# Elementwise work of GpSimd done by VectorE, in a two-layer retention / DeltaNet / expert-retrieval step

## The chip, the cores and the metric

One core of a Trainium2 chip. The metric is device time of one launch in microseconds (us). Engines are written as in the profile: PE (TensorE products), PEld (its weight loads), DVE (VectorE), ACT (ScalarE), POOL (GpSimd), SP (the engine whose queue issues most transfers).

## The reference

Two token streams, a prompt of 128 tokens and a sample of 512, pass two layers of width 1024 with shared weights. A layer is a mixer (layer 0: retention and a short convolution; layer 1: gated DeltaNet and a Conformer convolution) and an expert mixer with 16384 experts:

```
def peer_ffn(h, wq, keys, u_tab, v_tab):
    q = (x @ wq).reshape(T, H_P, 2, D_KEY // 2)
    s = jnp.einsum('thpd,hpnd->thpn', q, keys)
    s1, i1 = lax.top_k(s[:, :, 0], TOPK); s2, i2 = lax.top_k(s[:, :, 1], TOPK)
    cand_i = (i1[..., :, None] * N_KEYS + i2[..., None, :])      # 128 * i1 + i2
    top_s, sel = lax.top_k(cand_s, TOPK)
    eidx = jnp.take_along_axis(cand_i, sel, axis=-1)
    gates = jax.nn.softmax(top_s)
    ...
        act = jax.nn.gelu(jnp.einsum('td,tkd->tk', xt, u_tab[et]))
        return jnp.einsum('tk,tkd->td', gt * act, v_tab[et])
```

Each token takes 8 x 16 experts; u_tab and v_tab hold 16384 rows of 1024 float32. DeltaNet needs the inverse of a triangular matrix for each chunk and head.

## The kernel before

The prompt's tile and the last of the sample's four token tiles get their experts by rows: GpSimd gathers 128 rows of u_tab, then 128 of v_tab, one 512 KB indirect transfer each, five ahead, into a pool of six row buffers (`fetch`, L1203). VectorE multiplies each u row tile by h and sums it (L1227) and adds each weighted v row tile to `gacc` (L1237). This is `peer_gather`, a generator that is advanced step by step behind other work.

The sample's other three tiles (384 tokens) go against all experts on TensorE, in 128 blocks of 128 experts ("experts of i1 = e"; a block is called an expert e below). For precision an operand is split in a high part, copied by ScalarE (L1307), and a low part, the difference (L1308); a product is then three one-pass products. There are two parts: `acts` computes gelu(U h) of a block (24 products of 384 columns, the tile A, low part `ul`) and stores it in memory; the dense stage in `peer_dense` loads it again (`w`), multiplies it by the gates (L1451), splits it (`wh`, `wl`) and the block of v_tab (`vh`, `vl`), and adds 18 products of 512 columns to `dacc`. In layer 1 62 of the 128 blocks are "fused": their activation is computed in the dense stage (`wf`).

Before the dense stage the sample's tiles pass `peer_topk` (per head: a comparison L1179, a product L1181, a sum L1182) and `gate_matrix` (per four tokens one comparison of 128x512, L1288, and three of 128x128, L1299, on VectorE; 8 products G on TensorE). `acts` and the gather of the sample's last tile run behind these, and behind the prompt's odd mixer in layer 0. The dense stage follows when all `acts` are done.

What sets the order: outside of the dense stages a scheduler orders the instructions of an engine at build time; from top-k to the end of `acts` the order of POOL alone is kept as the program writes it (`manual_schedule`, L1394), and in the dense stages that of POOL, DVE and ACT (L1424). On the chip each engine takes its instructions strictly in that order. Before the change POOL's written order holds the row transfers and the odd blocks' low parts in one sequence.

The four lines that carry the change, as they stand before:

```
self.split(hi, lo, w, (self.nc.vector, self.nc.gpsimd)[j % 2])            # L433, wq pieces
G.tensor_tensor(v4(off), v4(e1), m4(M_OFF + d * len(LEVELS) + lv), op=OP.mult)   # L935
self.split(uh, ul, ur, self.nc.gpsimd if e % 2 else self.nc.vector)       # L1317
self.split(vh, vl, vr, G if e % 2 else V)                                 # L1450
```

Of the kernel before, what the change touches and what calls it, by code (L numbers as in the profile page):

```python
# [17 lines left out]
P = 128  # L18
# [66 lines left out]
class Kern:  # L85
# [35 lines left out]
    @contextmanager  # L121
    def using(self, **kw):
        """these attributes for a while"""
        old = {k: getattr(self, k) for k in kw}
        self.__dict__.update(kw)
        yield
        self.__dict__.update(old)

    def laned(self, gen, **kw):
        """a generator that runs with these attributes"""  # L130
        while True:
            with self.using(**kw):
                r = next(gen, self)
                kw = {k: getattr(self, k) for k in kw}
            if r is self:
                return
            yield
# [4 lines left out]
    def all_banks(self):  # L142
        """the banks of the lane that is through, too"""
# [15 lines left out]
    def mm(self, out, lhsT, rhs, start, stop):  # L159
        """a float32 product; background work goes in between at its rate"""  # L160
# [3 lines left out]
    def tick(self, us):  # L164
        """background work for a time that the foreground takes"""
# [18 lines left out]
    def phase(self, side="left", **n):  # L184
        """scratch memory of one phase; the next phase's takes its place"""
# [13 lines left out]
    def a2(self, st, name):  # L199
        """one value per channel and token of the stream, channels on partitions"""  # L200
# [28 lines left out]
    # ---------------------------------------------------------------- helpers  # L229
    def rsqrt(self, src, scale, n, name, post=1.0):  # L230
        """post * (src * scale + EPS) ** -0.5 on a [128, n] tile, by a Newton step."""
# [12 lines left out]
    def log1p_exp_neg(self, x, n, name):  # L244
        """log(1 + exp(-|x|)) on a [128, n] tile."""
# [20 lines left out]
    def bcast_cols(self, cols, name, out=None, bank=None):  # L266
        """[128, 8] per-channel columns -> [128, 1024], the same row on each partition."""
# [11 lines left out]
    # ---------------------------------------------------------------- constants  # L279
# [47 lines left out]
    # ---------------------------------------------------------------- modulation  # L327
# [6 lines left out]
    def modulation(self, l, part):  # L334
        """Columns of sh1, sc1 (part 0), ga1 (1), sh2, sc2 (2), ga2 (3), a step for 128 of them"""
# [30 lines left out]
    def load_c_rows(self, mw):  # L366
        """2 silu(c) of both streams, the same row on each partition"""
# [10 lines left out]
    # ---------------------------------------------------------------- norm, modulate, transpose  # L378
    def normed(self, st):
        """1 / rms of the rows of the token tiles, a column each"""  # L380
# [12 lines left out]
    def h_transposed(self, st, mod, alloc, rows=None):  # L393
        """modulated rmsnorm of x as 8 tiles [128 channels, T]"""
# [27 lines left out]
    def proj_t(self, st, hT, w):  # L422
        """[128 columns of w, T] in PSUM from a piece [128, 8 x 128]"""
# [6 lines left out]
    def split_piece(self, w, j):  # L430
        """a piece's two parts"""
        hi, lo = (self.ph[t][0].tile([P, D], F32R, tag=t, name=self.nm(t)) for t in ("wh", "wl"))
        self.split(hi, lo, w, (self.nc.vector, self.nc.gpsimd)[j % 2])  # L433
        return hi, lo

    def proj_split(self, h, w):
        """proj_t with both operands split"""
# [6 lines left out]
    def proj_n(self, st, hT, ws, it):  # L444
        """[128 tokens, 512] in PSUM from four pieces [128, 2 x 512]"""
# [7 lines left out]
    def out_proj(self, st, yT, w_out, ga, cs=range(KC), its=None):  # L453
        """x += ga * (y @ w_out); a step for the first half of the chunks cs"""
# [23 lines left out]
    def taps(self, out, src, w, T, order):  # L478
        """out += w[:, j] * src shifted by j - len(w) // 2, tokens outside of the stream being 0"""
# [14 lines left out]
    # ---------------------------------------------------------------- even mixer  # L494
    def even_setup(self, ctx):
# [21 lines left out]
        # decay of the prompt's keys towards the final states, per token and (dir, head)  # L517
# [8 lines left out]
    def decay(self, st, h):  # L526
        """both directions' decay of head h between tokens, by their distance"""
# [124 lines left out]
    def even_states(self, st, kT, v):  # L652
        """final states of the prompt, both directions"""
# [18 lines left out]
    # ---------------------------------------------------------------- odd mixer  # L672
# [13 lines left out]
    def odd_mixer(self, st, ph=None):  # L686
        nc, A = self.nc, self.A
        V, S, PE, G = nc.vector, nc.scalar, nc.tensor, nc.gpsimd
# [5 lines left out]
        if big:  # L694
            # x waits in memory for the end of the mixer; k and v take its place
# [4 lines left out]
        # conformer branch: its gated projection and, behind the rest, its convolution  # L700
# [19 lines left out]
        # gates  # L720
# [16 lines left out]
        # q, k, v: short convolution and silu (twice the value) with channels on partitions, then  # L737
        # per token tile: normalised q, k, v with tokens on partitions, q and k transposed too
# [81 lines left out]
    def conformer_products(self, ys, hc, T):  # L820
        """the same on the tensor engine, a diagonal matrix for each tap"""
# [50 lines left out]
    def gdn(self, st, kn, vn, qT, kT, gg, beta, zg, of, conf, out):  # L872
        nc = self.nc
        V, S, G = nc.vector, nc.scalar, nc.gpsimd
# [12 lines left out]
        def pre(d, it, res):  # L887
            """what the scan needs of a chunk: u, w^T, decayed q^T and k, the masked attention"""
# [29 lines left out]
            G.tensor_tensor(v4(x), v4(x), m4(M_INCL + d), op=OP.mult)  # L918
            yield
            # A and the attention  # L920
# [10 lines left out]
            # (I + A)^-1 by doubling of its diagonal blocks: X holds it, Y its transpose  # L931
            Y, X = self.vt("Y"), self.vt("Xi")
            for lv, bsz in enumerate(LEVELS):
                off = self.vt("off")
                G.tensor_tensor(v4(off), v4(e1), m4(M_OFF + d * len(LEVELS) + lv), op=OP.mult)  # L935
# [113 lines left out]
    def gdn_out(self, of, zg, its):  # L1049
        """o -> its norm, gate and transpose, in place: [128 channels of a head, (head, token)]"""  # L1050
# [21 lines left out]
    # ---------------------------------------------------------------- PEER  # L1072
    def peer_prep(self, st, l):
# [4 lines left out]
        if st.s:  # L1078
# [3 lines left out]
            for c in range(KC):  # L1082
                self.split(full[0][c], full[1][c], hT[c], (self.nc.vector, self.nc.gpsimd)[c % 2])
# [4 lines left out]
        for jg in range(4):  # L1088
# [3 lines left out]
            for j in range(4 * jg, 4 * jg + 4):  # L1092
                w = self.piece(A["wq"][l, j])
                b = self.proj_split(full, self.split_piece(w, j)) if st.s else self.proj_t(st, hT, w)
# [638 lines left out]
```

## Time and profile before

| what | us |
|---|---|
| median of 3 timed runs | 4401.43 (4391.63 to 4402.98) |
| span of the profiled execution, the only time recorded of it | 4406.5 |
| PE busy / DVE busy / POOL busy / ACT busy in it | 3868.7 / 3677.7 / 2411.8 / 1498.3 |

The times are device times of whole launches; the profile is one further execution, whose span reads 0.1% above the median. "Busy" is time in which an engine had an instruction running. An instruction's span in a timeline can overlap that of the next on its engine by some 0.1 us; where instructions follow one another without idle time, the distance of two starts is what one costs.

### The profile page before, as it was taken

The numbers are of one execution on the slowest core, as the hardware profiler recorded it, in microseconds if no ns is written. First come the engines' busy times: TensorE is split into PE (matmuls) and PEld (weight loads), VectorE is DVE, ScalarE is ACT, GpSimd is POOL, SyncE is SP. The second block draws the span as 40 slices with busy tenths as digits, with TensorE's granted clock in tenths as the row PEclk, the third lists the DMA queues.
The fourth block names the chain that finished last, engine by engine and source line by source line (L and its number), as shares of the span: only waits on it lengthen the run. The fifth ranks groups of instructions, "written<-read, shape, count | busy, mean of one in ns | idle before, by whom it ended". The sixth has DMA issues, their size and how long they took to land.

```text
span 4406.5 us, 56677 instructions
## 1 busy us (share of the span) xinstructions
PE 3868.7 (88%) x19422; PEld 3206.9 (73%) x19422; DVE 3677.7 (83%) x6843; ACT 1498.3 (34%) x2828; POOL 2411.8 (55%) x1520
## 2 busy tenths in 40 slices
PE   6797858899999998899998987887589989999997
PEld 4453547899998987677775456756579978888886
DVE  6568889998998656988887997659989978888888
ACT  2110131122774442233332253532224743333333
POOL 0126673686143754766655777425265247776664
PEclk9998878789999999999999989899899999999999
DMA  7548886886688788899987967237256699989994
GB/s 284 172 157 328 288 305 232 310 316 228 237 301 304 246 284 307 269 320 319 320 304 278 339 225 236 65 120 253 72 202 224 256 321 327 326 311 319 322 318 171
DMA packets 437040, 1158.45 MB, mean 263 GB/s; under 512 B 39440, under 2 KB 188048, under 8 KB 430352
## 3 DMA queue, kind: packets, MB, share of 16 engines
q1 hardware_dynamic: 282064, 591.69, 38.5%
q0 software_dynamic: 154688, 563.15, 36.3%
q8 instruction: 152, 2.49, 0.2%
q14 instruction: 136, 1.11, 0.1%
HBM read 1060.71 MB, written 93.98 MB: 262 GB/s over the span
## 4 chain that ended last, share of the span: by engine, by line
PE 31%; DVE 16%; issue 10%; POOL 3%; ACT 2%; DMA 2%; SPq 0%; DVEq 0%; POOLq 0%; ACTq 0%
PE dacc L161 14%; PE A L161 10%; DVE row L1227 3%; DVE gacc L1237 3%; POOL row L1203 2%; PE po L161 2%; PE G L161 1%; DVE wl L1308 1%; ACT wh L1307 1%; DMA row<-v,eid 1%; DMA row<-u,eid 1%; PE pt L161 1%; DVE ul L1308 1%; DVE eq L1179 1%; DVE o L1299 1%
## 5 line engine op out<-in xcount | busy, mean ns | idle before, releaser
L161 PE MATMUL A<-hHL,uh 128*128 128x384 f32 x4096 | 1110.4, 351 | 25.9 <-ACT uh L1307 25.7
L1203 POOL DMA_INDIRECT row<-v,eid x512 | 672.9, 1314 | 491.3 <-DVE gacc L1237 195.7
L1227 DVE SCALAR_TENSOR_TENSOR row<-row,hn 128x1024 f32<-128x1024 f32 x512 | 701.3, 1385 | 153.5 <-DMA row<-u,eid 151.8
L1203 POOL DMA_INDIRECT row<-u,eid x512 | 688.0, 1344 | 249.9 <-DVE row L1227 110.3
L161 PEld LDWEIGHTS A<-hHL,uh 128*128 128x128 f32 x4096 | 767.9, 196 | 40.0 <-ACT uh L1307 28.4
L1237 DVE SCALAR_TENSOR_TENSOR gacc<-row,gel,gacc 128x1024 f32<-128x1024 f32 x508 | 744.6, 1466 | 55.3 <-DMA row<-v,eid 50.6
L161 PE MATMUL A<-hHL,ul 128*128 128x384 f32 x2048 | 721.0, 353 | 65.4 <-DVE ul L1308 59.8
L1308 POOL TENSOR_TENSOR ul<-ur,uh 128x1024 fp32r<-128x1024 f32 x128 | 334.1, 2610 | 504.0 <-ACT uh L1307 456.0
L161 PE MATMUL dacc<-vh,wh 128*128 128x512 f32 x1536 | 458.7, 397 | 77.2 <-ACT wh L1307 77.1
L1308 POOL TENSOR_TENSOR vl<-vr,vh 128x1024 fp32r<-128x1024 f32 x128 | 355.3, 2776 | 267.9 <-ACT vh L1307 146.3
L161 PE MATMUL dacc<-vl,wh 128*128 128x512 f32 x1536 | 474.9, 392 | 1.3 <-POOL vl L1308 1.3
L161 PE MATMUL dacc<-vh,wl 128*128 128x512 f32 x1536 | 457.9, 390 | 7.9 <-DVE wl L1308 7.9
L1307 ACT CAST wh<-w 128x384 fp32r<-128x384 f32 (+1 forms) x226 | 133.0, 589 | 963.6 <-DVE w L1451 422.0
L161 PEld LDWEIGHTS A<-hHL,ul 128*128 128x128 f32 x2048 | 400.8, 196 | 79.1 <-DVE ul L1308 67.2
L161 PE MATMUL pt<-hT,w 128*128 128x128 f32 (+1 forms) x1664 | 395.6, 395 | 22.9 <-DMA w<-wq 11.6
L1307 ACT CAST uh<-ur 128x1024 fp32r<-128x1024 f32 x256 | 267.7, 1046 | 422.5 <-PE A L161 288.6
L161 PEld LDWEIGHTS dacc<-vh,wh 128*128 128x128 f32 x1536 | 282.1, 189 | 161.2 <-ACT wh L1307 110.6
L161 PEld LDWEIGHTS pt<-hT,w 128*128 128x128 f32 x1664 | 246.4, 199 | 164.6 <-issue 143.8
L161 PEld LDWEIGHTS dacc<-vh,wl 128*128 128x128 f32 x1536 | 287.7, 188 | 73.3 <-DVE wl L1308 11.4
L161 PEld LDWEIGHTS dacc<-vl,wh 128*128 128x128 f32 x1536 | 288.4, 188 | 60.4 <-POOL vl L1308 2.6
L1307 ACT CAST vh<-vr 128x1024 fp32r<-128x1024 f32 x256 | 267.2, 1044 | 4.5 <-DMA vr<-v 4.4
L1451 DVE TENSOR_TENSOR w<-w,gt 128x384 f32<-128x384 f32 x194 | 243.8, 1257 | 3.7 <-DMA w<-wd 3.7
(373 smaller groups left out, 6160.3 us busy)
## 6 DMA issues: line engine op xcount, KB each, us to landing
ur<-ut SPq DMA_DIRECT2D x256, 512.0 KB, 4.6
vr<-v SPq DMA_DIRECT2D x256, 512.0 KB, 6.7
gd<-gst SPq DMA_DIRECT2D x48, 1024.0 KB, 5.7
gt<-gd SPq DMA_DIRECT2D x96, 512.0 KB, 7.8
wd<-w SPq DMA_DIRECT2D x194, 192.0 KB, 3.8
w<-wd SPq DMA_DIRECT2D x194, 192.0 KB, 6.4
w<-ada_k SPq DMA_DIRECT2D x56, 512.0 KB, 6.4
w<-wq SPq DMA_DIRECT2D x48, 512.0 KB, 5.3
```

Source lines behind the costliest of these rows:

```text
L161: self.nc.tensor.matmul(out, lhsT, rhs, start=start, stop=stop)
L1179: V.tensor_tensor(eq, sf[:, h, :].unsqueeze(2).to_broadcast([P, TOPK, NSLOT]), self.iota50.unsqueeze(1).to_broadcast([P, TOPK, NSLOT]), op ...
L1203: self.nc.gpsimd.indirect_dma_start(out=t, out_offset=None, in_=table, in_offset=bass.IndirectOffsetOnAxis(ap=idx, axis=0))
L1227: V.scalar_tensor_tensor(u, u, 1.0, hn, op0=OP.mult, op1=OP.mult, accum_out=act[:, k:k + 1])
L1237: V.scalar_tensor_tensor(gacc, v, t[:, k:k + 1], gacc, op0=OP.mult, op1=OP.add)
L1299: V.tensor_scalar(o1, self.iota128, cols[:, 0, t:t + 1], cols[:, 2, t:t + 1], op0=OP.is_equal, op1=OP.mult)
L1307: self.nc.scalar.copy(hi, src)
L1308: (eng or self.nc.vector).tensor_tensor(lo, src, hi.bitcast(F32), op=OP.subtract)
L1451: V.tensor_tensor(w.rearrange("p (b t) -> p b t", t=TB), w.rearrange("p (b t) -> p b t", t=TB), g[:, :, e % GQ, :], op=OP.mult)
```

## The change

Every elementwise instruction of GpSimd is issued on VectorE, with the same operands and shapes. GpSimd keeps the row transfers and the plain transfers of the prompt's weights. `split` loses its engine argument. (The diff also empties docstrings and comments, which changes no instruction.)

```
-    def split(self, hi, lo, src, eng=None):
+    def split(self, hi, lo, src):
         self.nc.scalar.copy(hi, src)
-        (eng or self.nc.vector).tensor_tensor(lo, src, hi.bitcast(F32), op=OP.subtract)
+        self.nc.vector.tensor_tensor(lo, src, hi.bitcast(F32), op=OP.subtract)
...
-        self.split(hi, lo, w, (self.nc.vector, self.nc.gpsimd)[j % 2])
+        self.split(hi, lo, w)
...
-                self.split(full[0][c], full[1][c], hT[c], (self.nc.vector, self.nc.gpsimd)[c % 2])
+                self.split(full[0][c], full[1][c], hT[c])
...
-        self.split(uh, ul, ur, self.nc.gpsimd if e % 2 else self.nc.vector)
+        self.split(uh, ul, ur)
...
-                self.split(vh, vl, vr, G if e % 2 else V)
+                self.split(vh, vl, vr)
...
-            nc.gpsimd.tensor_tensor(eq, eq, ci[:, h, :].unsqueeze(1).to_broadcast([P, TOPK, NSLOT]), op=OP.mult)
+            V.tensor_tensor(eq, eq, ci[:, h, :].unsqueeze(1).to_broadcast([P, TOPK, NSLOT]), op=OP.mult)
...
-            G.tensor_tensor(v4(x), v4(x), m4(M_INCL + d), op=OP.mult)
+            V.tensor_tensor(v4(x), v4(x), m4(M_INCL + d), op=OP.mult)
...
-                G.tensor_tensor(v4(off), v4(e1), m4(M_OFF + d * len(LEVELS) + lv), op=OP.mult)
+                V.tensor_tensor(v4(off), v4(e1), m4(M_OFF + d * len(LEVELS) + lv), op=OP.mult)
```

Three places show what this does to the orders. In the dense stage of layer 0, DVE, an even and an odd block (`vl` the low part of the v block, `gacc` the gather's sum, `w` the gates' product). Before:

```order
L1308 TENSOR_TENSOR vl_15011<-vr_14865,vh_15010 128x1024
L1451 TENSOR_TENSOR w_14867<-w_14867,gt_14727 128x384
L1308 TENSOR_TENSOR wl_15016<-w_14867,wh_15015 128x384
L1237 SCALAR_TENSOR_TENSOR gacc_13277<-row_14869,gel_13274,gacc_13277 128x1024
L1451 TENSOR_TENSOR w_14901<-w_14901,gt_14727 128x384
L1308 TENSOR_TENSOR wl_15051<-w_14901,wh_15050 128x384
```

And of the change:

```order
L1308 TENSOR_TENSOR vl_15011<-vr_14865,vh_15010 128x1024
L1451 TENSOR_TENSOR w_14867<-w_14867,gt_14727 128x384
L1308 TENSOR_TENSOR wl_15016<-w_14867,wh_15015 128x384
L1237 SCALAR_TENSOR_TENSOR gacc_13277<-row_14869,gel_13274,gacc_13277 128x1024
L1308 TENSOR_TENSOR vl_15046<-vr_14899,vh_15045 128x1024
L1451 TENSOR_TENSOR w_14901<-w_14901,gt_14727 128x384
L1308 TENSOR_TENSOR wl_15051<-w_14901,wh_15050 128x384
```

The odd block's `vl` now stands on DVE ahead of its `w`; nothing else moved there.

POOL behind the prompt's odd mixer of layer 0, rows of u_tab (`u,eid`) for the sample's last tile. Before:

```order
L1203 DMA row_12738<-u,eid_4955 128x1024
L1203 DMA row_12787<-u,eid_4955 128x1024
L1203 DMA row_12790<-u,eid_4955 128x1024
L1308 TENSOR_TENSOR ul_12805<-ur_12753,uh_12804 128x1024
L1203 DMA row_12836<-u,eid_4955 128x1024
L1203 DMA row_12908<-u,eid_4955 128x1024
L1203 DMA row_12911<-u,eid_4955 128x1024
L1308 TENSOR_TENSOR ul_12929<-ur_12874,uh_12928 128x1024
```

And of the change:

```order
L1203 DMA row_12738<-u,eid_4955 128x1024
L1203 DMA row_12787<-u,eid_4955 128x1024
L1203 DMA row_12790<-u,eid_4955 128x1024
L1203 DMA row_12836<-u,eid_4955 128x1024
L1203 DMA row_12908<-u,eid_4955 128x1024
L1203 DMA row_12911<-u,eid_4955 128x1024
```

Before, every third row transfer stood behind a low part, which needs its block's `uh` from ScalarE; now the row transfers stand behind one another alone.

DVE in the gate matrix of layer 0 (`o` the comparisons of L1288 and L1299, `row,act` a gathered u row tile's product). Before:

```order
L1299 TENSOR_SCALAR o_1470_7087<-iota_98,gcols_6887 128x128
L1299 TENSOR_SCALAR o_1471_7090<-iota_98,gcols_6887 128x128
L1299 TENSOR_SCALAR o_1472_7093<-iota_98,gcols_6887 128x128
L1288 TENSOR_TENSOR o_1468_7084<-iota_98,gcols_6887 128x512
L1308 TENSOR_TENSOR ul_7461<-ur_7253,uh_7460 128x1024
L1299 TENSOR_SCALAR o_1476_7104<-iota_98,gcols_6887 128x128
L1299 TENSOR_SCALAR o_1477_7107<-iota_98,gcols_6887 128x128
L1299 TENSOR_SCALAR o_1478_7110<-iota_98,gcols_6887 128x128
L1288 TENSOR_TENSOR o_1474_7101<-iota_98,gcols_6887 128x512
```

And of the change, the same tokens:

```order
L1299 TENSOR_SCALAR o_1470_7087<-iota_98,gcols_6887 128x128
L1299 TENSOR_SCALAR o_1471_7090<-iota_98,gcols_6887 128x128
L1299 TENSOR_SCALAR o_1472_7093<-iota_98,gcols_6887 128x128
L1227 SCALAR_TENSOR_TENSOR row_10019,act_5108<-row_10019,hn_2873 128x1024
L1227 SCALAR_TENSOR_TENSOR row_10074,act_5108<-row_10074,hn_2873 128x1024
L1227 SCALAR_TENSOR_TENSOR row_10077,act_5108<-row_10077,hn_2873 128x1024
L1299 TENSOR_SCALAR o_1476_7104<-iota_98,gcols_6887 128x128
L1299 TENSOR_SCALAR o_1477_7107<-iota_98,gcols_6887 128x128
L1288 TENSOR_TENSOR o_1474_7101<-iota_98,gcols_6887 128x512
L1299 TENSOR_SCALAR o_1478_7110<-iota_98,gcols_6887 128x128
```

The scheduler has placed gathered row products among the comparisons that stood behind the gate matrix before. Counted in the whole order of layer 0, between the first and the last comparison of the gate matrix DVE has 21 row products and 12 `ul` before, and 95 and 34 of the change; between the first L1179 and the gate matrix 20 row products and 50 `gacc` before, 33 and 43 of the change; behind the gate matrix, up to the dense stage, 87 row products before and none of the change. On PE, 66.7 blocks of `acts` stand ahead of the gate matrix's last product before and 72.5 of the change, 44.9 and 41.1 ahead of its first.

## Rows read from the trace of the kernel before

**Rows 1.** The page, part 1: busy us of each engine, share of the span.
```profile
PE 3868.7 (88%) x19422; PEld 3206.9 (73%) x19422; DVE 3677.7 (83%) x6843; ACT 1498.3 (34%) x2828; POOL 2411.8 (55%) x1520
```

**Rows 2.** Stages: length; busy us, (instructions); granted clock, DMA share, GB/s.
```profile
811.00:1110.00 299.00, 280.59 (x1602) 278.37 (x1602) 267.62 (x448) 71.38 (x102) 216.51 (x119) 0.86 0.78 277
1110.00:1315.00 205.00, 193.21 (x1361) 187.90 (x1359) 199.20 (x458) 149.90 (x338) 63.11 (x36) 1.00 0.75 271
1315.00:1749.00 434.00, 405.62 (x2559) 386.83 (x2559) 294.66 (x736) 170.34 (x315) 213.95 (x140) 0.97 0.81 286
1749.00:2346.00 597.00, 538.19 (x2277) 421.41 (x2276) 524.94 (x477) 188.54 (x266) 378.47 (x191) 1.00 0.86 294
2605.00:2870.00 265.00, 210.03 (x1431) 180.71 (x1429) 195.66 (x245) 124.39 (x288) 164.59 (x123) 0.88 0.42 139
2960.00:3590.00 630.00, 510.84 (x2927) 474.72 (x2926) 577.49 (x1538) 270.92 (x525) 291.16 (x167) 0.92 0.61 212
3590.00:4395.00 805.00, 783.26 (x3773) 684.53 (x3771) 704.38 (x681) 275.91 (x399) 547.30 (x306) 1.00 0.87 303
```

**Rows 3.** Groups of POOL: busy us, mean ns | idle before, releaser.
```profile
L1308 POOL TENSOR_TENSOR vl<-vr,vh 128x1024 fp32r<-128x1024 f32 x128 | 355.3, 2776 | 267.9 <-ACT vh L1307 146.3 <-issue 116.3 <-DVE wl L1308 4.8
L1308 POOL TENSOR_TENSOR ul<-ur,uh 128x1024 fp32r<-128x1024 f32 x128 | 334.1, 2610 | 504.0 <-ACT uh L1307 456.0 <-PE G L161 27.9 <-PE A L161 20.1
L1181 POOL TENSOR_TENSOR eq<-eq,ci 128x800 f32<-128x800 f32 x80 | 166.3, 2081 | 119.4 <-DVE eq L1179 103.0 <-DVE eid L1187 11.8 <-DVE ci L1164 3.5
L935 POOL TENSOR_TENSOR off<-e,msk 128x512 f32<-128x512 f32 x70 | 102.7, 1484 | 34.3 <-PE bY L161 12.3 <-DVE hc L869 10.5 <-DVE e L928 6.3
```

**Rows 4.** Timeline, DVE, two blocks of layer 0: start us, us.
```profile
2000.57 0.56 DVE L1308 TENSOR_TENSOR wl<-w,wh 128x384 fp32r<-128x384 f32 x1 [0.62 <-ACT wh L1307]
...
2003.38 0.55 DVE L1451 TENSOR_TENSOR w<-w,gt 128x384 f32<-128x384 f32 x1
2004.55 0.56 DVE L1308 TENSOR_TENSOR wl<-w,wh 128x384 fp32r<-128x384 f32 x1 [0.62 <-ACT wh L1307]
2005.03 1.28 DVE L1237 SCALAR_TENSOR_TENSOR gacc<-row,gel,gacc 128x1024 f32<-128x1024 f32 x1
2006.22 2.80 DVE L1451 TENSOR_TENSOR w<-w,gt 128x384 f32<-128x384 f32 x1
2009.64 0.56 DVE L1308 TENSOR_TENSOR wl<-w,wh 128x384 fp32r<-128x384 f32 x1 [0.62 <-ACT wh L1307]
```

**Rows 5.** Timeline, POOL, the same stretch.
```profile
2005.60 3.00 POOL L1308 TENSOR_TENSOR vl<-vr,vh 128x1024 fp32r<-128x1024 f32 x1 [1.33 <-issue]
```

**Rows 6.** Timeline, PE, the same stretch.
```profile
2005.26 0.62 PE L161 MATMUL dacc<-vl,wh 128*128 128x512 f32 x2
...
2008.43 0.61 PE L161 MATMUL dacc<-vh,wl 128*128 128x512 f32 x2
```

**Rows 7.** Groups of DVE over the span.
```profile
L1227 DVE SCALAR_TENSOR_TENSOR row<-row,hn 128x1024 f32<-128x1024 f32 x512 | 701.3, 1385 | 153.5 <-DMA row<-u,eid 151.8 <-DVE row L1227 0.4
L1451 DVE TENSOR_TENSOR w<-w,gt 128x384 f32<-128x384 f32 x194 | 243.8, 1257 | 3.7 <-DMA w<-wd 3.7
...
L1308 DVE TENSOR_TENSOR wl<-wf,wh 128x384 fp32r<-128x384 f32 x62 | 166.8, 2690 | 41.5 <-ACT wh L1307 41.5
```

**Rows 8.** Timeline, DVE, gate matrix of layer 0.
```profile
1191.99 0.85 DVE L1299 TENSOR_SCALAR o<-iota,gcols 128x128 f32<-128x128 f32 x3
...
1193.36 1.22 DVE L1308 TENSOR_TENSOR ul<-ur,uh 128x1024 fp32r<-128x1024 f32 x1
...
1197.24 2.89 DVE L1299 TENSOR_SCALAR o<-iota,gcols 128x128 f32<-128x128 f32 x3
```

**Rows 9.** Timeline, POOL, the same stretch.
```profile
1196.60 2.95 POOL L1308 TENSOR_TENSOR ul<-ur,uh 128x1024 fp32r<-128x1024 f32 x1 [17.92 <-ACT uh L1307]
```

**Rows 10.** Waits of DVE, 1315 to 1749 us: total us, times, longest.
```profile
DVE row L1227 <- DMA row<-u,eid: 71.7, 42, 10.0
```

**Rows 11.** Waits, scan of layer 1 (2605 to 2870 us).
```profile
PE bY L492 <- DVE Xi L937: 26.0, 8, 6.9
```

More of the change, by code (lines that the diff above doesn't have):

```diff
@@ L428, in proj_t, with split_piece @@
         return b
-    def split_piece(self, w, j):
+    def split_piece(self, w):
         hi, lo = (self.ph[t][0].tile([P, D], F32R, tag=t, name=self.nm(t)) for t in ("wh", "wl"))
-        self.split(hi, lo, w, (self.nc.vector, self.nc.gpsimd)[j % 2])
+        self.split(hi, lo, w)
         return hi, lo
@@ L687, in odd_mixer @@
         nc, A = self.nc, self.A
-        V, S, PE, G = nc.vector, nc.scalar, nc.tensor, nc.gpsimd
+        V, S, PE = nc.vector, nc.scalar, nc.tensor
         T, nt = st.T, st.nt
@@ L873, in gdn @@
         nc = self.nc
-        V, S, G = nc.vector, nc.scalar, nc.gpsimd
+        V, S = nc.vector, nc.scalar
         nt = st.nt
@@ L1093, in peer_prep @@
                 w = self.piece(A["wq"][l, j])
-                b = self.proj_split(full, self.split_piece(w, j)) if st.s else self.proj_t(st, hT, w)
+                b = self.proj_split(full, self.split_piece(w)) if st.s else self.proj_t(st, hT, w)
                 q = self.a2(st, "q")
@@ L1358, in peer_dense @@
         nc, A = self.nc, self.A
-        V, S, PE, G = nc.vector, nc.scalar, nc.tensor, nc.gpsimd
+        V, S, PE = nc.vector, nc.scalar, nc.tensor
         tiles, gt = list(range(st.nt - 1)), st.nt - 1
```

## Prediction

> **What bounds the kernel now.** I read the busy times first: PE 88%, DVE 83%, POOL 55% [rows 1]. These are means over stages with different limits, so I cut the span into stages [rows 2] and asked in each which engine is full. Layer 0: in the top-k stage (811 to 1110 us) PE has 281 of 299 us and DVE 268; in the gate matrix (1110 to 1315) 193 and 199 of 205; in the prompt's odd mixer (1315 to 1749) PE has 406 of 434 and DVE only 295; in the dense stage (1749 to 2346) PE 538 and DVE 525 of 597. Layer 1: the scan (2605 to 2870) fills neither; split, top-k and gate matrix (2960 to 3590) fill DVE (577 of 630); the dense stage (3590 to 4395) fills PE (783 of 805).
>
> Then I looked at what a POOL instruction does to DVE. In the dense stage of layer 0 the gates' product `w` of an even block takes 0.55 us; that of the odd block starts at 2006.22, while POOL works on `vl` (2005.60 to 2008.60), and takes 2.80, to 2009.02 [rows 4, 5]. 2008.60 plus 0.55 is 2009.15, within 0.13: the short instruction runs when POOL's is over. In the gate matrix three comparisons take 0.85 us, and 2.89 when POOL's `ul` runs from 1196.60 to 1199.55 [rows 8, 9]. So DVE and POOL's elementwise work take turns, and much of DVE's busy time is waiting inside instructions: `w` over the span has a mean of 1257 ns against 550, `wl` of fused blocks 2690 against 560, the row product 1385 against about 1200 [rows 4, 7]. That is 194 x 0.71 = 137, 62 x 2.13 = 132 and 512 x 0.19 = 95 us, 364 together, without the groups not shown.
>
> **What the change moves.** POOL loses 128 `vl`, 128 `ul`, 80 `eq` products and 70 `off` masks [rows 3], and 34 smaller ones. On DVE a difference of 128x1024 takes 1.22 us [rows 8]; by width I take 0.96 for 800 columns and 0.65 for 512 (estimates, not above 1.22 nor below 0.55, the 384 columns of `w`). 256 x 1.22 + 80 x 0.96 + 70 x 0.65 + 34 x about 0.9 = 465 us are added, at least 364 given back: DVE's total hardly moves, so where the work comes to stand decides. Each wait is now for a smaller reason, but the order also changes: row transfers no longer stand behind POOL's `ul`, which waited for `uh` (504 us idle ahead of `ul` [rows 3]), and the scheduler has moved 74 more row products into the gate matrix of layer 0. By stage:
>
> Dense, layer 0. An even block's round on DVE is 3.98 us (`wl` at 2000.57 to `wl` at 2004.55), an odd one's 5.09 (to 2009.64) [rows 4]; the mean is 4.53. With its own `vl` the odd round becomes an even one, 3.98. PE needs 18 products at (2008.43 - 2005.26) / 14 = 0.226 us [rows 6], 4.08. PE then sets the pace. Transfers take 0.86 of the DMA engines now [rows 2], and would take 0.94 at the new pace; I take 4.12. The first 24 blocks stand beside the prompt's top-k: (597 - 104 x 4.53) / 24 = 5.2 us each, with eight more `eq` products and 12 more `vl` on DVE against what they blocked; I take no change. 104 x 0.41 = **-43**. Ends: -21, if transfers hold it at 4.33, and -55, if the first blocks gain too.
>
> Gate matrix, layer 0. One group of four tokens costs DVE 1.37 us (1191.99 to 1193.36) [rows 8], 96 groups 132. Before: 21 row products x 1.2 (the distance 2005.03 to 2006.22 of its sister `gacc` [rows 4]) = 25, 12 `ul` = 14, 12 stalls of 2.0 = 24, sum 195 of 205, rest 10. Now: 132 + 95 x 1.2 + 34 x 1.2 + 10 = 297, and I add 3 for late rows: 300, **+95**. The 74 transfers that come with them (POOL has nothing else to do there) bring 38 MB; with 55 MB now and 8 more blocks' loads that is about 99 MB in 300 us, 330 GB/s, above every stage of rows 2. Ends: +80 and +130.
>
> Top-k, layer 0. Added to DVE: 32 x 0.96 + 22 x 1.22 + 13 row products x 1.2 - 7 `gacc` x 1.2 = 65. Given back: 54 stalls, between 0.85 us (the 364 over 426 instructions) and 2.0 each; with DVE 90% busy most POOL instructions hit one, and I take 1.4, 75. The sum's hand-over from POOL is gone too: **-18** (ends -43, +20; PE has 3.8 blocks less here).
>
> Odd mixer, layer 0. PE is full, and has 61.3 - 55.5 = 5.8 blocks less to do, because they ran beside the long gate matrix: 5.8 x 24 products x 0.17 (0.226 by width) = 24 us. DVE loses 87 row products and their 71.7 us of waiting [rows 10], which PE's work covered: little comes of it. **-27** (ends -45, -15).
>
> Scan, layer 1. 56 masks and 8 others move to DVE, 64 x 0.65 = 42 us, against 64 stalls of some 0.65. On the chain a mask of 1.48 us [rows 3] becomes 0.65 once in each of seven levels, in two waves of chunks: 7 x 2 x 0.83 = 12; PE's 26 us behind `Xi` [rows 11] may shrink too. What is queued behind a mask on DVE is the next `gacc`, 1.28. **-12** (ends -25, +10).
>
> Split, top-k, gate matrix, layer 1. 32 x 0.96 + 33 x 1.22 + 12 x 1.1 = 84 added, 77 stalls x 1.2 = 92 back: **-8** (ends -45, +20). Here only a dozen row products change places.
>
> Dense, layer 1. PE has 22 us of idle time, no more can come: **-10** (ends -18, 0). DVE gets 95 x 1.2 = 114 and gets back the 132 of `wl` alone.
>
> What lies ahead of 811 us and between 2346 and 2605 moves next to nothing: **0**. Sum: -43 + 95 - 18 - 27 - 12 - 8 - 10 = -23. The profile's span is 4406.5, 5 us above the median of the runs; the difference is taken to the median: 4401 - 23 = **4378**.
>
> One rule speaks against the change. The Trainium skill, "Perfetto Trace Analysis", Optimizing Scalar/DVE Operations, says that offloading from a saturated DVE, even to GPSIMD, may make sense, and adds that the two share an SBUF read port, so that it might not help. By its first half the 465 us would simply lengthen the stages in which DVE is full; rows 4 and 5, where 3.00 us of POOL cost DVE 2.25, bear out the second half.
>
> **The rivals.**
> (A) Slower: the row products in the gate matrix wait for their rows. In the odd mixer 87 of them waited 71.7 us, 0.82 each [rows 10], beside idle time; in the gate matrix such a wait holds every comparison behind it. 95 x 0.82 = 78: the sum becomes +55, 4456. It decides from 0.38 us a row on (36 us). For it: 330 GB/s. Against it: rows now leave POOL at once, five ahead, one per 3 us.
> The Trainium skill, "SBUF — State Buffer", SBUF: two separate sides, has a rule that would feed this: a DVE instruction in a two-port mode keeps GPSIMD from writing the descriptors of its transfers. No row here shows such a stall.
> (B) The dense stages are held by transfers: 4.33 a block in layer 0 (-21 in place of -43) and nothing in layer 1: -23 + 22 + 10 = +9, 4410.
> (C) The gate matrix gives more back: ends of three terms, +80, -43, -45: -23 - 15 - 25 - 18 = -81, 4320. For it: PE's idle 28 us in the odd mixer.
> (D) DVE's long instructions are its own, and nothing is given back: +65, +119, +77 (64 x 1.2 in the dense stage), +42 and +84 by stage, less 27: +360, 4761. Rows 4, 5, 8 and 9 are against it.
>
> **How the numbers follow.** My forecast 0.50, A 0.18, B 0.13, C 0.17, D 0.02. The forecast's own range is 4348 to 4408. The range for 8 in 10 reaches from C's time into A's, 4318 to 4440. A measurement tells about 0.3%, 13 us. Faster: 0.38 of the forecast, C, 0.01 of B: 0.56. Same: 0.09 and 0.10 of B: 0.19. Slower: 0.03, A, 0.02 of B, D: 0.25.
>
> **What the profile after would show.** Right: `w` at 0.55 and `wl` at 0.56 in all blocks; 4.1 us a block in layer 0's dense stage with PE without gaps; a gate matrix of some 300 us in layer 0, full on DVE, with PE idle in it; DVE's total below 3700. Wrong: long instructions on DVE with no POOL work beside them; waits for `row<-u` in the gate matrix above 36 us; a gate matrix under 270 us; DMA share at its limit in the dense stages.

## The result, and the profile after

The changed kernel takes 4282.4 us (median of 4 runs, 4273.4 to 4289.4) against 4397.1 (4 runs): ratio 0.973, 95% interval 0.970 to 0.976. The medians are 115 us apart; the profiled execution has a span of 4287.3 us, 119.2 below that of before, and since stages can be read from profiles alone, I go by these 119 us. I had forecast 4378, with a range from 4318 up: the sign was right, the size far too small.

The page, part 1, of the changed kernel (busy us, share of the span):

```profile
PE 3831.8 (89%) x19422; PEld 3202.6 (75%) x19422; DVE 3467.9 (81%) x7283; ACT 1506.8 (35%) x2825; POOL 1475.3 (34%) x1080
```

DVE has 440 more instructions and 210 us less busy time than in [rows 1]. The stages, cut at the same events as in [rows 2]:

```profile
820.00:1092.00 272.00, 257.51 (x1536) 255.24 (x1537) 258.41 (x533) 67.48 (x96) 126.54 (x83) 0.89 0.92 331
1092.00:1372.00 280.00, 244.34 (x1543) 234.28 (x1542) 271.11 (x602) 161.88 (x352) 130.14 (x91) 0.95 0.93 341
1372.00:1763.00 391.00, 377.07 (x2456) 361.28 (x2455) 192.66 (x611) 161.45 (x305) 1.64 (x2) 0.99 0.58 189
1763.00:2295.00 532.00, 519.34 (x2274) 425.55 (x2272) 452.49 (x543) 192.97 (x256) 220.29 (x120) 1.00 0.94 329
2552.00:2787.00 235.00, 204.22 (x1451) 177.08 (x1450) 194.31 (x312) 126.41 (x293) 78.60 (x59) 0.92 0.48 158
2877.00:3485.00 608.00, 505.42 (x2923) 475.24 (x2922) 549.63 (x1617) 266.81 (x524) 118.22 (x90) 0.91 0.62 220
3485.00:4275.00 790.00, 779.71 (x3779) 682.16 (x3777) 623.48 (x769) 279.09 (x397) 306.39 (x212) 1.00 0.89 309
```

Only the second, the gate matrix of layer 0, became longer (205 to 280): DVE is full (271 of 280) and PE idle for 36 us. The stage behind it gives back 43. Groups of DVE over the span:

```profile
L1237 DVE SCALAR_TENSOR_TENSOR gacc<-row,gel,gacc 128x1024 f32<-128x1024 f32 x508 | 650.9, 1281 | 31.3 <-DMA row<-v,eid 27.6
L1227 DVE SCALAR_TENSOR_TENSOR row<-row,hn 128x1024 f32<-128x1024 f32 x512 | 612.9, 1222 | 62.2 <-DMA row<-u,eid 60.3
L1451 DVE TENSOR_TENSOR w<-w,gt 128x384 f32<-128x384 f32 x194 | 107.4, 554 | 3.7 <-DMA w<-wd 3.7
...
L1181 DVE TENSOR_TENSOR eq<-eq,ci 128x800 f32<-128x800 f32 x80 | 78.1, 990 | 0.0
...
L935 DVE TENSOR_TENSOR off<-e,msk 128x512 f32<-128x512 f32 x70 | 45.2, 688 | 0.0
...
L1308 DVE TENSOR_TENSOR wl<-wf,wh 128x384 fp32r<-128x384 f32 x62 | 34.6, 559 | 39.4 <-ACT wh L1307 39.4
```

Against [rows 7] `w` fell from 1257 to 554 ns and `wl` of fused blocks from 2690 to 559. `gacc` fell from 1466 to 1281, 94 us over its 508, a group I had left out of the sum. Two blocks of the dense stage of layer 0, the timeline of DVE (start us, us), beside [rows 4]:

```profile
2000.93 0.56 DVE L1308 TENSOR_TENSOR wl<-w,wh 128x384 fp32r<-128x384 f32 x1 [0.62 <-ACT wh L1307]
2001.40 1.28 DVE L1237 SCALAR_TENSOR_TENSOR gacc<-row,gel,gacc 128x1024 f32<-128x1024 f32 x1
2002.62 1.23 DVE L1308 TENSOR_TENSOR vl<-vr,vh 128x1024 fp32r<-128x1024 f32 x1
2003.76 0.55 DVE L1451 TENSOR_TENSOR w<-w,gt 128x384 f32<-128x384 f32 x1
2004.94 0.56 DVE L1308 TENSOR_TENSOR wl<-w,wh 128x384 fp32r<-128x384 f32 x1 [0.62 <-ACT wh L1307]
...
2009.02 0.56 DVE L1308 TENSOR_TENSOR wl<-w,wh 128x384 fp32r<-128x384 f32 x1 [0.62 <-ACT wh L1307]
```

The odd block now takes an even block's time: 4.01 and 4.08 us from one `wl` to the next, where they were 3.98 and 5.09. Waits of DVE in the gate matrix (1092 to 1372 us): total, times, longest.

```profile
DVE row L1227 <- DMA row<-u,eid: 3.0, 3, 1.9
```

95 waits of 0.82 us were rival A's price; DVE waited 3.0 us in all. The rows came in time.

### The profile page after: what moved, and what is told of

It is laid out like the page before. It is cut to its first block, busy times and chain, and to the rows that moved or that the text cites. A ratio compares the mean times of both kernels' runs of the same rounds, so it can differ in the third digit from the quotient of the medians.

```text
span 4287.3 us, 56379 instructions
## 1 busy us (share of the span) xinstructions
PE 3831.8 (89%) x19422; PEld 3202.6 (75%) x19422; DVE 3467.9 (81%) x7283; ACT 1506.8 (35%) x2825; POOL 1475.3 (34%) x1080
## 4 chain that ended last, share of the span: by engine, by line
PE 63%; DVE 16%; issue 7%; DMA 4%; POOL 3%; ACT 1%; SPq 0%; DVEq 0%; POOLq 0%; ACTq 0%
PE dacc L161 23%; PE A L161 20%; PE pt L161 7%; DVE row L1227 3%; POOL row L1203 3%; PE G L161 2%; PE mod L347 2%; PE po L161 2%; PE cy L161 1%; DVE o L1299 1%; DMA row<-u,eid 1%; DMA row<-v,eid 1%; DVE gacc L1237 1%; DVE ul L1308 1%; DVE o L1288 1%
## 5 line engine op out<-in xcount | busy, mean ns | idle before, releaser
L1203 POOL DMA_INDIRECT row<-v,eid x512 | 745.5, 1456 | 1460.6 <-DVE gacc L1237 713.2
L1203 POOL DMA_INDIRECT row<-u,eid x512 | 700.3, 1368 | 1048.6 <-DVE row L1227 641.3
L1237 DVE SCALAR_TENSOR_TENSOR gacc<-row,gel,gacc 128x1024 f32<-128x1024 f32 x508 | 650.9, 1281 | 31.3 <-DMA row<-v,eid 27.6
L1227 DVE SCALAR_TENSOR_TENSOR row<-row,hn 128x1024 f32<-128x1024 f32 x512 | 612.9, 1222 | 62.2 <-DMA row<-u,eid 60.3
L161 PE MATMUL dacc<-vh,wh 128*128 128x512 f32 x1536 | 480.4, 394 | 31.4 <-ACT wh L1307 31.3
L1308 DVE TENSOR_TENSOR ul<-ur,uh 128x1024 fp32r<-128x1024 f32 x256 | 312.7, 1223 | 166.6 <-ACT uh L1307 166.4
L161 PE MATMUL dacc<-vh,wl 128*128 128x512 f32 x1536 | 391.2, 390 | 0.0
L1308 DVE TENSOR_TENSOR vl<-vr,vh 128x1024 fp32r<-128x1024 f32 x256 | 313.2, 1224 | 72.2 <-ACT vh L1307 69.8
L1308 DVE TENSOR_TENSOR wl<-w,wh 128x384 fp32r<-128x384 f32 (+1 forms) x226 | 147.0, 652 | 110.8 <-ACT wh L1307 110.6
```

The source lines that it names most:

```text
L161: self.nc.tensor.matmul(out, lhsT, rhs, start=start, stop=stop)
L1203: self.nc.gpsimd.indirect_dma_start(out=t, out_offset=None, in_=table, in_offset=bass.IndirectOffsetOnAxis(ap=idx, axis=0))
L1227: V.scalar_tensor_tensor(u, u, 1.0, hn, op0=OP.mult, op1=OP.mult, accum_out=act[:, k:k + 1])
L1237: V.scalar_tensor_tensor(gacc, v, t[:, k:k + 1], gacc, op0=OP.mult, op1=OP.add)
L1308: self.nc.vector.tensor_tensor(lo, src, hi.bitcast(F32), op=OP.subtract)
```

## The experiments

My theory (theory 1 in the expectations): DVE and GpSimd take turns at elementwise work, so what GpSimd does costs DVE about as much as doing it itself would, or more; the 119 us are these stalls less the added work, and beside that the change moved the row products to a worse place. Rivals: GpSimd's results only came late to those who wait for them (hand-over); or the order of the instructions made the gain.

The table has the lengths of stages in us, from each profiled execution, between the starts of the same instructions: first `eq` of layer 0's sample, first and last one-hot comparison (L1299), first and last `w` of the dense stage; last row product to last `cy` of layer 1's mixer; layer 1's first `wl` to its first dense `w`. So some differ by up to 23 us from the windows above. The first mixers, up to the split of layer 0, vary from 584 to 604 us among these executions, which is why I compare stages. Of the totals I compare ratios to before, with their 95% intervals.

| run | top-k 0 | gate 0 | odd mixer 0 | sum of three | dense 0 | scan 1 | split to gate 1 | ratio |
|---|---|---|---|---|---|---|---|---|
| before | 304 | 200 | 435 | 940 | 594 | 243 | 628 | 1 |
| changed | 276 | 276 | 391 | 943 | 528 | 212 | 606 | 0.973 (0.970-0.976) |
| e1 pace | 243 | 240 | 464 | 946 | 516 | 211 | 613 | 0.976 (0.973-0.979) |
| e2 idle subtraction | 274 | 275 | 391 | 941 | 619 | 211 | 608 | 0.994 (0.991-0.996) |
| e3 `vl` back | 272 | 275 | 391 | 938 | 586 | 210 | 607 | 0.985 (0.982-0.989) |
| e4 `ul` back | 264 | 214 | 449 | 928 | 528 | 208 | 612 | 0.973 (0.970-0.976) |
| e5 masks back | 274 | 202 | 434 | 911 | 528 | 238 | 608 | 0.973 (0.970-0.976) |
| e6 `eq` back | 276 | 277 | 407 | 959 | 538 | 209 | 627 | 0.986 (0.983-0.988) |
| e7 idle copy | 273 | 275 | 391 | 939 | 565 | 209 | 608 | 0.978 (0.975-0.981) |
| e8 `ul` of layer 0 back | 260 | 212 | 449 | 921 | 528 | 211 | 608 | 0.969 (0.966-0.972) |
| e9 pace, 72 blocks | 251 | 237 | 435 | 923 | 528 | 209 | 607 | 0.966 (0.963-0.969) |
| e10 prompt's masks back | 274 | 207 | 433 | 915 | 528 | 206 | 604 | 0.963 (0.961-0.966) |
| e11 before, `vl` moved | 301 | 200 | 429 | 930 | 538 | 244 | 629 | 0.985 (0.982-0.989) |
| e12 idle in the scan | 271 | 274 | 391 | 937 | 528 | 235 | 606 | 0.977 (0.974-0.980) |

### Idle work on GpSimd: e2, e7, e12

The edits are shown against the changed kernel, cut to the lines that matter; what stands behind `#` is mine.

```diff
                 self.split(vh, vl, vr)
+                if l == 0 and e & 1:
+                    nc.gpsimd.tensor_tensor(st.hn, st.hn, st.hn, op=OP.subtract)   # e2
+                    nc.gpsimd.tensor_copy(st.hn, st.hn)                            # e7, in its place
```

e2. 

> All of the change stays; in the dense stage of layer 0, each odd block gets one GpSimd subtraction of 128x1024 on a tile that is no longer read (`hn`, from itself), so no instruction waits for it. The order on DVE is that of the changed kernel. Theory 1 (turn-taking): each of the 64 costs DVE up to 2.25 us in the instruction that meets it; DVE has 458 of 531 us there, so up to 64 x 2.25 = 144 are added, and the stage goes to 458 + 144 = 602 at most, 570 to 602: 4282 + 40 to 70 = 4320 to 4350, with `w` or `vl` of about 3 us in odd blocks. Rival (hand-over: what cost time was that `vl` and `ul` of GpSimd came 1.5 us later than DVE's; a product that nobody waits for costs nothing): 4282, within 5, and no long instruction on DVE.

e7. 

> As the run e2, but each of the 64 idle pieces of GpSimd work is a copy of 128x1024 with one operand (`hn` onto itself) in place of a subtraction with two. If all elementwise work of GpSimd takes turns with DVE: the dense stage of layer 0 goes from 528 towards 619 us as in e2, and `wl` of odd blocks takes 2 us: 4282 + 97 = 4379, less in the ratio of the two durations. Rival (only two-operand work of GpSimd takes turns with DVE's): 4282, within 6, `wl` at 0.56.

e2 took the dense stage from 528 to 619 us and the kernel to 4379.1. DVE's timeline and then GpSimd's in e2, one odd block, and the group of `wl` in that stage (a mean of 1242 ns, where it was 559):

```profile
2007.19 2.08 DVE L1308 TENSOR_TENSOR wl<-w,wh 128x384 fp32r<-128x384 f32 x1 [0.62 <-ACT wh L1307]
```

```profile
2006.94 1.90 POOL L1452 TENSOR_TENSOR hn<-hn 128x1024 f32<-128x1024 f32 x1
```

```profile
L1308 DVE TENSOR_TENSOR wl<-w,wh 128x384 fp32r<-128x384 f32 x126 | 156.5, 1242 | 70.6 <-ACT wh L1307 70.6
```

GpSimd's instruction ends at 2008.84, `wl` at 2009.27, 0.43 later: it ran when the other was through. 56 of the 64 odd blocks read like this one; the instruction that was met is `wl`, not the `w` or `vl` of my expectation. Nobody waits for `hn`, so hand-over cannot be the cause here; 64 x (2.08 - 0.56) = 97 is near the 91 that the stage lost. The stage went past my upper bound of 602, which let the stalls fill DVE's idle time; that idle time (72 us in the changed kernel, 70 in e2) is the 0.62 that DVE waits for `wh` in every block, and it stays. In e7 (4312.9 us) the same block reads, DVE and then GpSimd:

```profile
2007.03 1.20 DVE L1308 TENSOR_TENSOR wl<-w,wh 128x384 fp32r<-128x384 f32 x1 [0.63 <-ACT wh L1307]
```

```profile
2006.76 1.05 POOL L1452 COPY hn<-hn 128x1024 f32<-128x1024 f32 x1
```

A copy takes turns too: it ends at 2007.81, and `wl` 0.42 later, as in e2. Its price is 64 x 0.64 = 41 (measured 36), less than in the ratio of the two durations, because both pieces start some 0.26 us ahead of `wl` and only what is left of them counts. The rival, that only two-operand work of GpSimd counts, falls. The Trainium skill, "SBUF — State Buffer", Who interferes with whom, says that a DVE instruction with two SBUF inputs contends with a GpSimd instruction that reads SBUF. `wl` has two inputs, and both idle pieces read: the rows of e2 and e7 agree.

```diff
                 V.tensor_tensor(v4(off), v4(e1), m4(M_OFF + d * len(LEVELS) + lv), op=OP.mult)
+                if st.s:
+                    nc.gpsimd.tensor_tensor(st.hn[:, :512], off, off, op=OP.subtract)
```

e12. 

> All of the change stays; in layer 1's mixer, behind each of the 56 masked products `off` on DVE, GpSimd makes one idle subtraction of 128x512 of `off` from itself, onto a tile that is no longer read, and nothing waits for it but the buffer of `off`. The masks' own length on the chain of the inversion stays 0.69 us. If the scan gained because GpSimd's masks held DVE (and their queue the row transfers), most of the 31 us comes back: scan 211 to 230 or more, 4282 + 20 = 4302. Rival (the gain was the mask's shorter length and hand-over on the chain, 1.48 against 0.69 us and no semaphore between two engines): scan 211 to 215, 4282 to 4286.

The scan went to 235, the kernel to 4309.2. Two groups of DVE in e12's scan, in the changed kernel 1283 and 689 ns:

```profile
L1239 DVE SCALAR_TENSOR_TENSOR gacc<-row,gel,gacc 128x1024 f32<-128x1024 f32 x65 | 97.9, 1507 | 11.3 <-DMA row<-v,eid 10.7 <-DVE off L935 0.2
L935 DVE TENSOR_TENSOR off<-e,msk 128x512 f32<-128x512 f32 x56 | 49.0, 917 | 0.0
```

Work off the chain takes away 23 of the 31 us that the scan had gained. The masks' own length and hand-over, on which my forecast had rested, are left with about 8, if the idle pieces cost DVE what the masks did; PE's waits for a mask, 12.3 us before and 3.8 after, say the same.

### One part undone, or done alone: e3, e4, e5, e6, e11

`split` gets its engine argument again in e3 and e4.

```diff
-                self.split(vh, vl, vr)
+                self.split(vh, vl, vr, nc.gpsimd if e % 2 else V)        # e3
...
-        self.split(uh, ul, ur)
+        self.split(uh, ul, ur, self.nc.gpsimd if e % 2 else self.nc.vector)   # e4
...
-            V.tensor_tensor(v4(x), v4(x), m4(M_INCL + d), op=OP.mult)
+            nc.gpsimd.tensor_tensor(v4(x), v4(x), m4(M_INCL + d), op=OP.mult)   # e5, and L935 alike
...
-            V.tensor_tensor(eq, eq, ci[:, h, :].unsqueeze(1).to_broadcast([P, TOPK, NSLOT]), op=OP.mult)
+            nc.gpsimd.tensor_tensor(eq, eq, ci[:, h, :].unsqueeze(1).to_broadcast([P, TOPK, NSLOT]), op=OP.mult)   # e6
```

e3. 

> From the changed kernel, the `vl` subtractions of odd blocks go back to GpSimd (128), all else stays. Theory 1: the dense stage of layer 0 goes back from 531 to about 590 us (4.54 a block), that of layer 1 gains at most 5 (PE 788 of 793, DVE 626 - 78 + 60 of stalls): 4282 + 60 = 4342, ratio to before 0.986. Rival (the dense stage gained from the row transfers or from the start that the other moves gave it): under 4310.

It took 4337.0: `vl` alone is worth 1.2% (54 us), all of it in layer 0's dense stage (528 to 586).

e11, the same part alone, on the kernel before:

```diff
-                self.split(vh, vl, vr, G if e % 2 else V)
+                self.split(vh, vl, vr, V)
```

> From the kernel before, `vl` of the odd blocks alone (128) goes to DVE, all else stays on GpSimd. By the dense stage of layer 0 (594 to about 535: 3.98 to 4.08 us a block in the steady part) and nothing in layer 1 (there `ul` still takes turns, and PE has 12 us of idle time): 4401 - 58 = 4343, ratio 0.987. Rival (the parts of the change need each other: the `ul`, `eq` and masks that stay take the gain): above 4370.

It took 4340.5 against 4407.9. This part does not need the others; I had missed 11 us in layer 1's dense stage (790 to 780 between first and last `w`).

e4. 

> From the changed kernel, the `ul` subtractions of odd blocks go back to GpSimd (128), and with them the order of the rows before the change (17 + 20 row products up to the end of the gate matrix). Theory 1: it costs 128 stalls of 1 to 2 us less 128 x 1.22 of DVE work; in layer 0 the better order gives back what the stalls take: top-k, gate matrix and odd mixer 943 to 930, layer 1's top-k + 15, dense + 5: 4282 + 5, from 4270 to 4300. Against e1, which has the same order without stalls, + 30 (15 to 45). Rival (order alone): as e1 within 6 us. Rival (the gain came from `ul`, which left GpSimd's queue and no longer held the rows): above 4320.

It took 4284.4, as the changed kernel: a loss and a gain that cancel. But e4 was no slower than e1, which has the same row order and no stalls of `ul`; that part of the expectation (+30) failed, and e1 and e9 below show why.

e5. 

> From the changed kernel, the 70 products with a mask of the inversion's levels (`off`) and the 10 of `X` go back to GpSimd, all else stays. Theory 1, with GpSimd's queue in it (a mask stands behind a row transfer that waits for DVE's sum `gacc`, and DVE is held by the masks in turn): the scan of layer 1 goes back from 211 to 243 us, the rest stays: 4282 + 31 = 4313, from 4304 to 4322. Rival (the masks cost only their own length on the chain, 7 levels x 2 x 0.83 us): 4294, at most 4300.

The scan did what the theory said (212 to 238), the total did not (4287.2): layer 0's three stages fell from 943 to 911. I had overlooked that the prompt's 16 masks (14 `off`, 2 `X`) stand in GpSimd's written order and hold the row transfers behind them.

e6. 

> From the changed kernel, the 80 lookup products `eq` go back to GpSimd, all else stays. Theory 1: DVE loses 0.99 us of work for each and gets a stall of about 1.35 us (74 us over 55 GpSimd instructions in the top-k stage of before), and its sum waits for GpSimd: 32 x 0.36 + 15 = 26 in each top-k stage, 8 x 0.4 in the dense stage of layer 0: 4282 + 50 = 4332, from 4310 to 4345. Rival (the top-k stages gained from `ul`'s leaving GpSimd): 4290 at most. Since the run with `ul` back on GpSimd had shorter top-k stages, I give the rival little.

It took 4345.0, at the upper end: ratio 0.986, 56 us. The top-k stages did not lengthen; PE had 30 us of idle time in layer 0's, not 15, did fewer blocks there, and the odd mixer (+15), layer 1's gate matrix (+24) and layer 0's dense stage (+10) paid. DVE has 80 instructions (78 us) less to do than in the changed kernel and its busy time is 9 us longer, 3477.1 against 3467.9, so stalls are there; but its sums also wait 17.8 us for GpSimd's `eq`. No run separates the two in this class: that its 56 us are turns alone is not shown.

Undone one by one, the four classes cost 54, 1, 0 and 56 us. That the sum, 111, comes near the 119 is partly luck: the 1 of `ul` and the 0 of the masks are each a loss by stalls and a gain by the order of the rows. The 24 halves of `wl` and `hf` were not tried.

### Where the row products stand: e1, e8, e9, e10

```diff
+            if un is not None and i % 2 == 0:            # e1; e9: l == 0 and i % 2 == 0 and i < 72
+                self.nc.gpsimd.tensor_tensor(self.small([P, 8], "pace"), un[0][:, :8].bitcast(F32),
+                                             un[0][:, :8].bitcast(F32), op=OP.subtract)
             w = up.tile([P, wd.shape[2]], F32, tag="w", name=self.nm("w"))
```

e1. 

> All of the change stays; in the runs over the blocks of layer's act products, each second block gets one GpSimd subtraction of 8 columns that reads its `uh` and whose result nobody uses, so that the row transfers behind it in GpSimd's order come as late as before. DVE's order then has 17 + 26 row products up to the end of the gate matrix of layer 0, not 40 + 88. Theory 1 (turn-taking, and DVE is full in the gate matrix): the gate matrix of layer 0 falls from 273 to about 200 us (132 for the comparisons, 26 x 1.2 + 24 x 1.2 = 60, rest 8), the odd mixer rises from 391 to about 440, since PE must do the blocks that it did beside the long gate matrix; PE's idle time over the three stages falls from 62 to about 36: 4282 - 26 = 4256, ratio to before 0.968. Rival (the change gained by its order, because rows no longer stood behind `ul`): the gain in the odd mixer goes, 4300 to 4330. Rival (place of the rows does not matter): 4282, within 5.

It took 4292.9, no gain: by that run alone the place of the rows does not matter. But the stages are not those expected. PE's longest wait in e1's odd mixer, and what DVE does at its end:

```profile
PE dacc L161 <- ACT wh L1307: 39.0, 1, 39.0
```

```profile
1754.71 0.99 DVE L1181 TENSOR_TENSOR eq<-eq,ci 128x800 f32<-128x800 f32 x1
1755.73 0.99 DVE L1182 TENSOR_REDUCE ef<-eq 128x16 f32<-128x800 f32 x1
1756.75 0.23 DVE L1187 CAST eid<-ef 128x128 int32<-128x128 f32 x1
1756.90 1.22 DVE L1308 TENSOR_TENSOR vl<-vr,vh 128x1024 fp32r<-128x1024 f32 x1
1758.03 0.55 DVE L1454 TENSOR_TENSOR w<-w,gt 128x384 f32<-128x384 f32 x1
```

The scheduler had put the prompt's eight lookups of layer 1 (L1179 to L1187) ahead of the first `vl` and `w`, and PE, out of other work, stood behind them. In the changed kernel they run among the first blocks of the dense stage.

e8 (in `acts`, `ul` of each second block to GpSimd if `l == 0`). 

> From the changed kernel, `ul` of each second block of layer 0 alone (64) goes back to GpSimd; layer 1's stay on DVE. From the stages of e4: top-k, gate matrix and odd mixer of layer 0 take 928 us where the changed kernel takes 943, and the parts in which e4 lost (gate matrix of layer 1, +18) stay as they are: 4282 - 15 = 4267, ratio to before 0.9695. Rival (e4's shorter odd mixer is an accident of one profile): 4282, within 5.

e9. 

> As e1 (8 columns of GpSimd work behind `uh`, so that the row transfers come as late as before), but only in layer 0 and only in the first 72 act blocks. DVE's order has the same 17 + 26 row products up to the end of the gate matrix as e1, and the prompt's 8 lookup sums stand behind the first `w` of the dense stage again, as in the changed kernel, and not ahead of it. If e1 failed because of those sums (PE waited 39 us for the first `wh` behind them), the three stages take 946 - 39 + 12 = 919 where the changed kernel takes 943, the lookups cost the dense stage the 12 us that e1 had saved there (516 to 528), and layer 1 stays: 4282 - 24 = 4258, ratio to before 0.967. Rival (where the rows stand does not matter, e1 showed it): 4282, within 6.

e10 (the edit of e5, with `V if st.s else nc.gpsimd`). 

> From the changed kernel, the masks of the prompt in layer 0 alone (14 `off`, 2 `X`) go back to GpSimd; those of layer 1 stay on DVE. In GpSimd's order these masks hold the row transfers behind them: 40 + 27 row products up to the end of the gate matrix of layer 0, 61 in the odd mixer. From the stages of e5: top-k, gate matrix and odd mixer 911 where the changed kernel takes 943, and layer 1's scan at 211 as in the changed kernel: 4282 - 32 = 4250, ratio 0.965. Rival (place of the rows does not matter): 4282, within 6.

e8 took 4271.4: the sum of three stages fell to 921, but its interval overlaps the changed kernel's. e9 took 4260.5 (expected 4258). Its rows stand as in e1 up to the end of the gate matrix and its lookups behind the first `w` again; the three stages take 923 where e1 took 946, and PE's wait is

```profile
PE dacc L161 <- ACT wh L1307: 10.1, 1, 10.1
```

e4, too, which holds the rows back in all blocks and has the lookups behind the first `w`, takes 928. So the lookups took the gain from e1's three stages. They are not the whole difference of 32 us between the two runs: the dense stage gives 12 of the 23 back, and layer 1, which e9 leaves alone and e1 paces too, takes 9 more in e1 up to its last `w`. e10 took 4249.9 (expected 4250), ratio 0.963: it beats both kernels. That the number was met so closely is luck: its six runs spread from 4236.7 to 4257.2. Its three stages, as windows:

```profile
825.00:1096.00 271.00, 258.02 (x1528) 255.28 (x1529) 259.47 (x534) 67.02 (x95) 128.80 (x83) 0.89 0.92 331
1096.00:1307.00 211.00, 199.60 (x1379) 197.53 (x1378) 191.11 (x469) 150.64 (x338) 28.36 (x21) 0.97 0.72 261
1307.00:1740.00 433.00, 411.06 (x2622) 393.28 (x2621) 275.45 (x728) 174.81 (x322) 117.07 (x88) 0.98 0.76 265
```

PE's busy time over the three is 869 us here and 879 in the changed kernel's; its idle time is 46 us, not 64. GpSimd stood still for 266 us, until 1423.87, ahead of the first of the prompt's masks, which the remaining 61 transfers of u rows stand behind; this wait holds their row products out of the gate matrix:

```profile
POOL X L918 <- ACT dl L912: 265.8, 1, 265.8
```

## Why the prediction was wrong in size

| stretch | forecast | measured |
|---|---|---|
| ahead of 811 us | 0 | +9 |
| top-k, layer 0 | -18 | -27 |
| gate matrix, layer 0 | +95 | +75 |
| odd mixer, layer 0 | -27 | -43 |
| dense, layer 0 | -43 | -65 |
| 2346 to 2605 | 0 | -2 |
| scan, layer 1 | -12 | -30 |
| split, top-k, gate matrix, layer 1 | -8 | -22 |
| dense, layer 1 | -10 | -15 |
| tail | 0 | +1 |
| sum | -23 | -119 |

No term had the wrong sign, but the sum missed 96 us, more than rival C's three better ends (58): 22 in the dense stage of layer 0, 20 in the gate matrix, 18 in the scan, 16 in the odd mixer, 14 in layer 1's split to gate matrix.

**The step that failed** is "465 us are added, at least 364 given back: DVE's total hardly moves". DVE's busy time fell by 210 us. By the means of all groups, before and after, some 615 came back, not 364. (615 less 465 is 150; the other 60 are overlaps of neighbouring spans, which busy time counts once.) I had priced three groups and let the rest go unpriced: `gacc` (94 us), the comparisons `o` (413 to 351 ns over 576, 36), the lookup comparison `eq` (1438 to 990 over 80, 36), `ul` itself (1409 to 1223 over 128, 24), `Xi` and `hf`. A lower bound stood in for the size, and it set the lower end of my price of a stall (0.85 us, by 426 instructions; there are 440, and it would be 0.83). Of the 210, 72 lie in layer 0's dense stage, 81 in layer 1's, where PE is full, and 28 in layer 1's split to gate matrix. In layer 0's top-k (-9) and the scan (-1) DVE's busy time moved as I had it; there I mis-sized waits.

**Dense, layer 0.** Mechanism right (e2, e3, e11). The steady blocks came to 3.99 to 4.08 us, not 4.12; PE has 13 us of gaps where it had 59, though the transfers reached a share of 1.0 between 1870 and 2150 us, the sign that I had named for rival B: it did not bind. The first 24 blocks, for which I "take no change", gained 17; with the prompt's `eq` on GpSimd (e6, e11) or with `vl` there (e3) they are 10 slower again.

**Gate matrix, layer 0.** 88 row products and 32 `ul` where I had 95 and 34: 9 x 1.2 = 11 of the 20 us, which is no gain, since the seven row products stand in the top-k stage instead. The work-by-width sum was otherwise good, and late rows cost the 3 us that I had given them. I called its sign rightly; that it could be avoided at so little cost (e9, e10) I had not seen.

**Top-k, layer 0.** I let seven `gacc` leave this stage and did not look where they went: the split ahead of it has 84 instead of 77, the +9. DVE's busy time fell by 9 us, where I had 10, though seven more row products came in. Its idle time fell from 31 to 14, where I had allowed 8 for the hand-over; before, its sums stood behind GpSimd's `eq` for

```profile
DVE ef L1182 <- POOL eq L1181: 11.4, 7, 1.7
```

**Odd mixer, layer 0.** "Little comes of it" was wrong: besides the 28 us of PE work that left (24 forecast), 14 of PE's 28 us of idle time went, what rival C had named. No run singles out which wait that was.

**Scan and lookups, layer 1.** For the scan I set 42 us of masks against 42 of stalls, which held for DVE's busy time, and kept only the masks' length on the chain. But stalls also delay what the chain needs next: e12 shows them, and what queues behind them, as 23 of the 31 us. In split to gate matrix, e6 loses 21 of the 22 us again (606 to 627, 628 before), so `eq` is the class that the -8 had too cheap; how much of it is stalls and how much hand-over stays open.

## What to carry to other kernels

Price an elementwise instruction on a helper engine by what it does to the busy engine's instructions beside it, in every group that shrinks, not only the conspicuous ones: an idle GpSimd subtraction of 1.90 us cost DVE 1.5. When work leaves an in-order queue, ask what else it was holding back there: `ul` and the masks had kept the row products out of a stage in which DVE is full, and giving GpSimd 16 small masks back was worth 1%. An experiment that fails by its total may still be right in its stages; look for the wait that took the gain (39 us in e1) before dropping the theory.

## What was not expected of the hardware

Between DVE's work and GpSimd's transfers only one side waits. GpSimd's row transfers do not hold DVE: the two-operand `vl` has a mean of 1223 ns where one runs beside most of it and 1225 where none does. But the transfers are longer beside DVE's two-operand work: over the changed kernel's trace they take 939 ns beside no DVE work (46 of them) and 1533 where such work covers over 70% of them (675). Spans on GpSimd are rough, but these stand clearly apart; no experiment varied this alone, so the cause is read from what stands side by side. Its timeline at the end of the gate matrix; DVE makes row products until 1349.55 and comparisons from there on:

```profile
1345.32 1.68 POOL L1203 DMA_INDIRECT row<-v,eid  x1 [5.85 <-DVE row L1227]
1347.30 1.99 POOL L1203 DMA_INDIRECT row<-v,eid  x1 [0.30 <-issue]
1349.60 0.94 POOL L1203 DMA_INDIRECT row<-v,eid  x1 [0.30 <-issue]
```

The prediction said that no row shows transfers held by DVE; these do show them slowed, by two-operand work and not by the two-port mode of the rule named there. It cost little where rows are fetched five ahead: DVE waited 3.0 us for rows in this gate matrix. The Trainium skill, "SBUF — State Buffer", Who interferes with whom, infers that a two-operand DVE instruction does not hold up descriptor generation; the measurement here says that a row transfer beside one takes 1.6 times as long.
